# Larger pieces, shared key tiles and late stores in a NaN-ignoring row maximum

## The chip, the cores and the metric

One core of one Trainium2 chip. The metric is the device time of one execution in microseconds (us), the median of the runs given. A difference counts as "faster" or "slower" from 2% on. The span in a profile is about 1.8 us shorter than the device time.

## The reference

```python
# x: 32 x 2048 x 2048 float32, about 10% of it NaN
def reference(x, axis):          # axis = -1
    return np.nanmax(x, axis=axis).astype(np.float32)
```

65,536 rows of 2048 numbers, 8 KB each: 536.87 MB are read, 0.26 MB written. The 128 partitions take 512 rows each.

## The kernel before

A **tile** is 7 rows per partition (7.34 MB) in one of three rotating buffers `xt`. The sync engine (SP) issues its load. Each tile is worked in **pieces** of a few rows: ScalarE (ACT) turns the upper 16 bits of each number into a key in which NaN sorts lowest, into a tile `kt`; GpSimd (POOL), or for a few pieces ACT itself ("back", a minus sign in the list), turns the keys back into numbers in `xt`; VectorE (DVE) takes the maximum of the rows (`reds`). The next load of a buffer waits until DVE has read all of it. The lists in `TILES` give, per tile, the loads, the pieces and the maxima in rows; towards the end they get smaller (the **taper**). A group of tiles shares one result tile and one store.

```python
TILES = (
    [([1], [1], [1])]
    + [([7], [1, 2, 2, -1, 1], [1, 2, 2, 2])] * 59
    # ... 9 tiles of the taper cut
    + [([1, 3, 3], [1, 1, 1, 1, 2, -1], [1, 2, 1, 3])]
    # ... 3 cut
    + [([1, 1, 1, 1, 1, 1, 1], [1, 1, -1, 1, 1, 1, -1], [1, 2, 1, 1, 1, 1])]
)
GROUPS = [TILES[:7]] + [TILES[i : i + 6] for i in range(7, 73, 6)] + [TILES[73:]]
# ... pools: io bufs=3 (xt), mid bufs=4 (kt), res bufs=3 (acc, fin)
        for loads, pieces, reds in g:
            xt = io.tile([P, WIDE * D], i32, tag="xt")
            for c in loads:
                nc.sync.dma_start(out=xt[...], in_=xg[...])
            if len(stores) > 1:
                nc.sync.dma_start(**stores.pop(0))      # a store between two loads
            for c in pieces:
                kt = mid.tile([P, PIECE * D], u16, tag="kt")
                nc.scalar.activation(out=kt, in_=..., func=ACT.Prelu, ...)   # key
                # back on ACT (c < 0) or on POOL
                # ... and every maximum whose rows are complete:
                    nc.vector.tensor_reduce(out=acc[...], in_=xt[...], op=ALU.max)
        # ... end work of the group: none, fin; its store is appended to `stores`
    for st in stores:
        nc.sync.dma_start(**st)
```

Of the kernel before, what the change touches and what calls it, by code (L numbers as in the profile page):

```python
# [1 line left out]

# [4 lines left out]




TILES = (
    [([1], [1], [1])]
    + [([7], [1, 2, 2, -1, 1], [1, 2, 2, 2])] * 59
    + [([7], [2, 2, 1, 2], [4, 1, 2])]
    + [([7], [1, 2, 2, -2], [3, 2, 2])]
    + [([7], [1, 2, 2, 2], [3, 2, 2])]
    + [([7], [2, 2, 2, -1], [2, 2, 2, 1])]
    + [([2, 5], [1, 1, 2, 2, 1], [1, 1, 2, 2, 1])]
    + [([4, 3], [2, -2, 1, 1, 1], [2, 3, 2])]  # L20
    + [([4, 3], [2, 2, 2, -1], [2, 2, 3])] * 3
    + [([1, 3, 3], [1, 1, 1, 1, 2, -1], [1, 2, 1, 3])]
    + [([3, 2, 2], [1, 1, 1, 1, 1, 1, 1], [2, 1, 1, 1, 1, 1])]
    + [([2, 1, 2, 1, 1], [1, 1, -1, 1, 1, 1, 1], [3, 2, 1, 1])]
    + [([1, 1, 1, 1, 1, 1, 1], [1, 1, -1, 1, 1, 1, 1], [3, 1, 1, 1, 1])]
    + [([1, 1, 1, 1, 1, 1, 1], [1, 1, -1, 1, 1, 1, -1], [1, 2, 1, 1, 1, 1])]
)

GROUPS = [TILES[:7]] + [TILES[i : i + 6] for i in range(7, 73, 6)] + [TILES[73:]]
WIDE = 7  # L30
PIECE = 2



TOP = 0x7F7F
NAN = 0x7FC0
LOW = -129

EDGE = TOP + 0.25

NONE = -255.0 * 2.0**120


@with_exitstack
def kernel(
    ctx: ExitStack,
    tc: tile.TileContext,
    x: bass.AP,
    axis: bass.AP,
    out: bass.AP,  # L50
):









    nc = tc.nc
    P = nc.NUM_PARTITIONS
    f32, i32 = mybir.dt.float32, mybir.dt.int32
    i16, u16 = mybir.dt.int16, mybir.dt.uint16
    ALU = mybir.AluOpType
    ACT = mybir.ActivationFunctionType

    nd = len(x.shape)
    assert axis in (-1, nd - 1), axis
    D = x.shape[-1]  # L70

    xr = x.bitcast(i32).flatten_outer_dims()
    R = xr.shape[0]
    of = out.bitcast(i32).flatten_outer_dims().rearrange("r c -> (r c)")
    rows = [sum(sum(loads) for loads, _, _ in g) for g in GROUPS]
    assert R == P * sum(rows)

    io = ctx.enter_context(tc.tile_pool(name="io", bufs=3))
    mid = ctx.enter_context(tc.tile_pool(name="mid", bufs=4))
    res = ctx.enter_context(tc.tile_pool(name="res", bufs=3))  # L80
    sing = ctx.enter_context(tc.tile_pool(name="sing", bufs=1))
    flag = ctx.enter_context(
        tc.tile_pool(name="flag", bufs=2, space=bass.MemoryType.PSUM)
    )
    top = sing.tile([P, 1], f32)
    nc.vector.memset(top, EDGE)  # L86
    warm = sing.tile([P, 1], f32)
    nc.scalar.activation(out=warm, in_=top, func=ACT.Prelu, alpha=0.5)  # L88

    stores = []  # L90
    r0 = 0
    for s, g in zip(rows, GROUPS):
        xg = xr[r0 : r0 + P * s].rearrange("(p s) d -> p (s d)", p=P)
        og = of[r0 : r0 + P * s].rearrange("(p s) -> p s", p=P)
        r0 += P * s
        acc = res.tile([P, s], f32, tag="acc")
        base = 0
        for loads, pieces, reds in g:
            assert sum(loads) == sum(abs(c) for c in pieces) == sum(reds)
            xt = io.tile([P, WIDE * D], i32, tag="xt")  # L100
            at = 0
            for c in loads:
                nc.sync.dma_start(  # L103
                    out=xt[:, at * D : (at + c) * D],
                    in_=xg[:, (base + at) * D : (base + at + c) * D],
                )
                at += c
            if len(stores) > 1:
                nc.sync.dma_start(**stores.pop(0))
            at = done = 0  # L110
            reds = list(reds)
            for c in pieces:
                back, c = c < 0, abs(c)
                xp = xt[:, at * D : (at + c) * D]
                kt = mid.tile([P, PIECE * D], u16, tag="kt")
                nc.scalar.activation(  # L116
                    out=kt[:, : c * D],
                    in_=xp.bitcast(i16)[:, 1::2],
                    func=ACT.Prelu,
                    bias=top,  # L120
                    scale=-1.0,
                    alpha=float(TOP - LOW) / (EDGE - NAN),
                )
                if back:
                    nc.scalar.activation(  # L125
                        out=xp.bitcast(i16)[:, 1::2],
                        in_=kt[:, : c * D],
                        func=ACT.Copy,
                        bias=float(TOP),
                        scale=-1.0,  # L130
                    )
                else:
                    nc.gpsimd.tensor_scalar(  # L133
                        out=xp.bitcast(i16)[:, 1::2],
                        in0=kt[:, : c * D],
                        scalar1=-1.0,
                        scalar2=float(TOP),
                        op0=ALU.mult,
                        op1=ALU.add,
                    )  # L140
                at += c
                while reds and done + reds[0] <= at:
                    n = reds.pop(0)
                    nc.vector.tensor_reduce(  # L144
                        out=acc[:, base + done : base + done + n],
                        in_=xt[:, done * D : (done + n) * D]
                        .bitcast(f32)
                        .rearrange("p (c d) -> p c d", c=n),
                        axis=mybir.AxisListType.X,
                        op=ALU.max,  # L150
                    )
                    done += n
            base += at
        none = flag.tile([P, s], i32, tag="none")
        nc.vector.tensor_scalar(  # L155
            out=none,
            in0=acc,
            scalar1=NONE,
            scalar2=float(0x00C00000),
            op0=ALU.is_equal,  # L160
            op1=ALU.mult,
        )
        fin = res.tile([P, s], i32, tag="fin")
        nc.vector.tensor_tensor(  # L164
            out=fin, in0=acc.bitcast(i32), in1=none, op=ALU.bitwise_or
        )
        stores.append(dict(out=og, in_=fin))
    for st in stores:
        nc.sync.dma_start(**st)


# [1 line left out]
_INS = ['x', 'axis']  # L173
_OUTS = [((32, 2048), 'float32')]

_NUMBERS = {'axis': -1}


# [26 lines left out]
```

## Time and profile before

| | before |
|---|---|
| device time, median of 3 | 1262.26 us (1262.21 to 1262.27) |
| span of the profiled run | 1260.4 us, 1707 instructions |
| DMA engines taken by the main queue | 98.9% of the span |
| busy: DVE, ACT, POOL | 1127.1, 1123.5, 1063.1 us |
| maxima, keys, backs on ACT, backs on POOL | 292, 368, 70, 298 |

The first thing to read is that all three compute engines are 84 to 89% busy and yet none of them is the bound: the DMA row is. A second thing is read from the chain of waits: how long a buffer is **held** after its load has landed (24.1 us), since that decides when its next load can be issued.

### The profile page before, as it was taken

What the parts mean: (1) busy time and instruction counts of PE and PEld (TensorE: products, weight loads), DVE (VectorE), ACT (ScalarE), POOL (GpSimd) and SP (SyncE); (2) the same over time, 40 slices, a digit from 0 to 9 for tenths busy, and PEclk for the clock granted to TensorE, in tenths of its full rate; (3) what the DMA queues carried; (4) which work ended last, traced back from release to release, by engine and by line L of the source; (5) the groups of instructions that cost most, each with busy time, mean ns of one, the idle gap of its engine ahead of it and who ended that gap; (6) DMA issues with size and microseconds to landing.
All of it is one profiled execution on the core that took longest, in us unless ns stands there. A gap on an engine that the chain in (4) does not pass through costs nothing.

```text
span 1260.4 us, 1707 instructions
## 1 busy us (share of the span) xinstructions
DVE 1127.1 (89%) x319; ACT 1123.5 (89%) x440; POOL 1063.1 (84%) x302
## 2 busy tenths in 40 slices
DVE  1899998988989998988999898898989879999999
ACT  4888998888899889889889888998888889899997
POOL 2888888888888888888888888888888888998996
DMA  9999999999999999999999999999999999999995
GB/s 412 437 437 437 435 433 417 434 437 437 436 435 435 427 424 437 436 435 437 435 434 424 426 437 435 437 437 433 435 416 437 437 436 437 417 433 430 425 422 211
DMA packets 16141, 537.25 MB, mean 426 GB/s; under 512 B 3456, under 2 KB 3456, under 8 KB 3456
## 3 DMA queue, kind: packets, MB, share of 16 engines
q1 hardware_dynamic: 16128, 537.14, 98.9%
q14 instruction: 13, 0.11, 0.0%
HBM read 536.87 MB, written 0.26 MB: 426 GB/s over the span
## 4 chain that ended last, share of the span: by engine, by line
DMA 52%; POOL 15%; ACT 13%; DVE 10%; issue 9%; SPq 0%; ACTq 0%; DVEq 0%
DMA xt<-in_x_dram 52%; POOL xt L133 15%; ACT kt L116 12%; DVE acc L144 10%; ACT xt L125 1%; SPq L103 0%; DVE none L155 0%; ACTq L116 0%; DVEq L144 0%; DVE fin L164 0%; ACTq L125 0%
## 5 line engine op out<-in xcount | busy, mean ns | idle before, releaser
L144 DVE TENSOR_REDUCE acc<-xt 128x2 f32<-128x4096 f32 (+2 forms) x292 | 1122.9, 3889 | 129.3 <-POOL xt L133 129.2
L133 POOL TENSOR_SCALAR xt<-kt 128x2048 int16<-128x2048 uint16 (+1 forms) x298 | 1062.9, 3567 | 189.1 <-ACT kt L116 175.7
L116 ACT ACTIVATE kt<-xt,top 128x2048 uint16<-128x2048 int16 (+1 forms) x368 | 951.1, 2657 | 128.4 <-DMA xt<-in_x_dram 128.4
L125 ACT ACTIVATE xt<-kt 128x2048 int16<-128x2048 uint16 x70 | 177.8, 2540 | 0.3
L155 DVE TENSOR_SCALAR none<-acc 128x42 int32<-128x42 f32 (+2 forms) x13 | 2.6, 202 | 0.5
L164 DVE TENSOR_TENSOR fin<-acc,none 128x42 int32<-128x42 int32 (+2 forms) x13 | 2.6, 197 | 0.4
L88 ACT ACT_TABLE_LOAD x1 | 1.3, 1283 | 0.7 <-PEq L186 0.7
L86 DVE MEMSET top<- 128x1 f32 x1 | 0.1, 59 | 0.8 <-PEq L186 0.8
L186 POOL MEMSET const-float32-0.0<- 128x1 f32 x1 | 0.1, 98 | 0.2 <-issue 0.2
L88 ACT ACTIVATE warm<-top 128x1 f32<-128x1 f32 x1 | 0.2, 203 | 0.0
L186 POOL MEMSET const-bfloat16-1.0<- 128x1 bf16 x1 | 0.1, 101 | 0.0
L186 POOL MEMSET const-uint8-127<- 128x1 uint8 x1 | 0.1, 101 | 0.0
L186 POOL MEMSET const-float32-1.0<- 128x1 f32 x1 | 0.1, 98 | 0.0
## 6 DMA issues: line engine op xcount, KB each, us to landing
xt<-in_x_dram SPq DMA_DIRECT2D x63, 7168.0 KB, 26.7
xt<-in_x_dram SPq DMA_DIRECT2D x7, 3072.0 KB, 25.6
xt<-in_x_dram SPq DMA_DIRECT2D x19, 1024.0 KB, 20.8
xt<-in_x_dram SPq DMA_DIRECT2D x4, 4096.0 KB, 19.6
xt<-in_x_dram SPq DMA_DIRECT2D x5, 2048.0 KB, 27.5
xt<-in_x_dram SPq DMA_DIRECT2D x1, 5120.0 KB, 23.2
out_dram<-fin SPq DMA_DIRECT2D x11, 21.0 KB, 26.5
out_dram<-fin SPq DMA_DIRECT2D x1, 21.5 KB, 26.7
```

Source lines behind the costliest of these rows:

```text
L86: nc.vector.memset(top, EDGE)
L88: nc.scalar.activation(out=warm, in_=top, func=ACT.Prelu, alpha=0.5)
L116: nc.scalar.activation(out=kt[:, : c * D], in_=xp.bitcast(i16)[:, 1::2], func=ACT.Prelu, bias=top, scale=-1.0, alpha=float(TOP - LOW) / (E ...
L125: nc.scalar.activation(out=xp.bitcast(i16)[:, 1::2], in_=kt[:, : c * D], func=ACT.Copy, bias=float(TOP), scale=-1.0,)
L133: nc.gpsimd.tensor_scalar(out=xp.bitcast(i16)[:, 1::2], in0=kt[:, : c * D], scalar1=-1.0, scalar2=float(TOP), op0=ALU.mult, op1=ALU.add,)
L144: nc.vector.tensor_reduce(out=acc[:, base + done : base + done + n], in_=xt[:, done * D : (done + n) * D] .bitcast(f32) .rearrange("p (c d ...
L155: nc.vector.tensor_scalar(out=none, in0=acc, scalar1=NONE, scalar2=float(0x00C00000), op0=ALU.is_equal, op1=ALU.mult,)
L164: nc.vector.tensor_tensor(out=fin, in0=acc.bitcast(i32), in1=none, op=ALU.bitwise_or)
L186: nc = _bacc.Bacc("TRN2", target_bir_lowering=False, num_devices=1)
```

## The change

Its intent is to halve the instructions and to take the stores out of the stream of loads. Up to the taper a tile is worked in two pieces of 3 and 4 rows, all turned back by POOL; the key tile holds 4 rows and may be shared by several small pieces, with two buffers instead of four; the 13 groups become 6; all stores are issued behind the last load. Two tiles (the 54th and 55th of seven rows) get lists of their own with a 5-row and a 7-row maximum. Cut to its core:

```diff
-    + [([7], [1, 2, 2, -1, 1], [1, 2, 2, 2])] * 59
+    + [([7], [3, 4], [3, 4])] * 53
+    + [([7], [-1, 3, -1, 2], [5, 2])]
+    + [([7], [4, 2, -1], [7])]
+    + [([7], [3, 4], [3, 4])] * 6
     # ... taper rewritten, same number of tiles
-GROUPS = [TILES[:7]] + [TILES[i : i + 6] for i in range(7, 73, 6)] + [TILES[73:]]
-PIECE = 2
+GROUPS = [TILES[:14]] + [TILES[i : i + 12] for i in range(14, 74, 12)]
+KEYS = 4
 # ...
-            if len(stores) > 1:
-                nc.sync.dma_start(**stores.pop(0))
 # ...
-                kt = mid.tile([P, PIECE * D], u16, tag="kt")
+                if used + c > KEYS:
+                    kt = mid.tile([P, KEYS * D], u16, tag="kt")
+                    used = 0
+                kp = kt[:, used * D : (used + c) * D]
+                used += c
```

(mid goes from 4 to 2 buffers, res from 3 to 1 with a tag per group.)

## The prediction

> **What bounds the kernel now.** I read the page first (the row of bytes moved, the landing times of the transfers), then the groups of instructions by shape, then the waits of the DMA queue, the chain that ended last, and the end of the timeline.
>
> The row of GB/s, of 40 equal slices:
>
> ```profile
> GB/s 412 437 437 437 435 433 417 434 437 437 436 435 435 427 424 437 436 435 437 435 434 424 426 437 435 437 437 433 435 416 437 437 436 437 417 433 430 425 422 211
> ...
> q1 hardware_dynamic: 16128, 537.14, 98.9%
> ...
> xt<-in_x_dram SPq DMA_DIRECT2D x63, 7168.0 KB, 26.7
> ```
>
> The reader is to see a transfer that is never short of work: the 16 DMA engines are taken for 98.9% of the span, and no slice but the first and the last is below 416. 536.87 MB at 437 GB/s are 1228.5 us, of a span of 1260.4. No compute engine can win time in the middle; what is left is the start, a few dips, and the last slice. In the trace's packet records a 7-row load lands every 16.94 us (7.34 MB, 433 GB/s), a store between two loads costs about 0.1 us, and some dips are isolated slow packets (2.1 us in sum). The last load lands near 1244.1.
>
> By shape, the durations that I use:
>
> ```profile
> L144 DVE TENSOR_REDUCE acc<-xt 128x2 f32<-128x4096 f32 x199 | 873.3, 4416 | 95.9 <-POOL xt L133 95.9
> L133 POOL TENSOR_SCALAR xt<-kt 128x4096 int16<-128x4096 uint16 x142 | 676.9, 4767 | 79.5 <-ACT kt L116 73.3
> L116 ACT ACTIVATE kt<-xt,top 128x4096 uint16<-128x4096 int16 x144 | 525.2, 3694 | 8.5 <-DMA xt<-in_x_dram 8.5
> L116 ACT ACTIVATE kt<-xt,top 128x2048 uint16<-128x2048 int16 x224 | 438.2, 1991 | 119.9 <-DMA xt<-in_x_dram 119.9
> L133 POOL TENSOR_SCALAR xt<-kt 128x2048 int16<-128x2048 uint16 x156 | 386.0, 2475 | 109.6 <-ACT kt L116 102.4
> L144 DVE TENSOR_REDUCE acc<-xt 128x1 f32<-128x2048 f32 x83 | 187.9, 2277 | 23.8 <-POOL xt L133 23.8
> L125 ACT ACTIVATE xt<-kt 128x2048 int16<-128x2048 uint16 x68 | 168.3, 2475 | 0.2
> L144 DVE TENSOR_REDUCE acc<-xt 128x3 f32<-128x6144 f32 x9 | 58.9, 6548 | 3.3 <-POOL xt L133 3.2
> ```
>
> Differences of one and two rows give, as an estimate, for n rows: ACT key 0.29 + 1.70n us, POOL way back 0.18 + 2.29n, DVE maximum 0.14 + 2.14n (6.55 at 3 rows, as measured). A piece saved is thus worth only 0.29, 0.18 or 0.14 us.
>
> The chain (start, length) and the queue's own waits:
>
> ```profile
> 80.38 26.64 DMA xt<-in_x_dram
> 107.09 5.61 ACT kt L116 x2
> 131.18 27.00 DMA xt<-in_x_dram
> ...
> SPq L103 <- DVE acc L144: 950.8, 59, 24.1
> SPq L103 <- DVE none L155: 186.6, 11, 21.3
> ```
>
> A load lands at 107.0, and the load that reuses its buffer is issued at 131.2: a tile occupies its buffer for **24.1 us after landing**. With three buffers two other loads, 33.9 us, move meanwhile. From issue to landing are 26.7 us, of which 16.94 are the load's own packets and about 1.3 its start (1.0, below) and its signal (0.3): it queued 8.5 us. That is the margin before the transfer runs dry.
>
> The end:
>
> ```profile
> 1242.32 15.38 DVE L144 TENSOR_REDUCE acc<-xt 128x1 f32<-128x2048 f32 x6
> ...
> 1257.93 0.16 DVE L164 TENSOR_TENSOR fin<-acc,none 128x7 int32<-128x7 int32 x1
> ```
>
> DVE works without a pause to 1257.7, 13.6 us after the last landing: a backlog, not the shortest way of one row, which is 2.0 + 2.5 + 2.3 = 6.8 us. Then 0.36 us of end work and 2.3 us for the last store.
>
> **What the Trainium skill says.** "DMA: Bandwidth & Descriptors", Specifications: 435 GB/s is the fabric's ceiling; the trace agrees (437 in the best slices). The same page, Latency and other measured facts: about 0.6 us to the first byte for a transfer issued by the sync engine; the trace's first load, issued at 0.74, moves its first packet at 1.75, so I use 1.0. "ScalarE: Activation LUTs", What ACT_TABLE_LOAD costs: 280 ns + 0.833 ns per element where the bias is a per-partition operand; the trace agrees (1991 and 3694 ns against 1986 and 3692), so 3 and 4 rows are 5.40 and 7.10. "SBUF — State Buffer", Who interferes with whom: tensor_reduce never contends with GpSimd for the shared port on trn2; the trace agrees, POOL's one-row form takes as long at the end, where DVE never rests, as in the middle. So I leave the durations as they are when both engines are fuller.
>
> **The change, part by part.**
>
> *Fewer pieces.* Counted from the lists: keys 368 to 188, copies back on ACT 70 to 15, POOL 298 to 173, maxima 292 to 166. ACT: 188 x 0.29 + 512 rows x 1.70 + 15 x 2.48 = 963 us (1129 in the groups now). POOL now returns 497 of 512 rows: 173 x 0.18 + 497 x 2.29 = 1170 (1063 now), 93%. DVE: 166 x 0.14 + 512 x 2.14 = 1118 (1123 now). All of it lies beside the transfer: directly 0 us.
>
> *The steady tile* (pieces 3, 4; time from its landing; 0.05 per handover). ACT 3 rows to 5.5, 4 rows to 12.6. POOL 3 rows 5.55 to 12.6, 4 rows 12.65 to 22.0. DVE 3 rows 13.8 (when the tile before is done) to 20.4, 4 rows 22.05 to **30.75**. POOL is busy 16.5 of 16.94 us per tile and frees the second key buffer at 22.0 - 16.94 = 5.06, just before ACT wants it at 5.5. The next load of this buffer moves at 30.75 + 0.05 + 1.0 = 31.8; the DMA is free for it at 33.88 - 0.3 = 33.55. So the margin falls from 8.5 to **1.75 us**, but holds: 0 us.
>
> *Two odd tiles*, the 54th and 55th of seven rows, break it. The order of instructions as built has in the first of them key 1, key 3, back 1, key 1, key 2, back 1 on ACT, ending at 17.95. The 5-row maximum needs that last copy: 18.0 to 28.8, the 2-row one to 33.25. Its buffer's next load moves at 34.3 instead of 33.55: 0.75 lost. In the second, ACT starts 1.0 late, 4 rows to 8.1; POOL 8.15 to 17.5, then 2 rows to 22.3; one 7-row maximum (15.1 us) waits for all: 22.35 to **37.45**. The next load moves at 38.5; the DMA has been free since 33.55 + 0.75 = 34.3: another 4.2 lost. The two tiles after it stay ahead of the late load. Sum: **+5.0 us** of idle DMA, which nothing later can recover, since the transfer has no slack.
>
> *Stores.* Ten that lay between loads go behind the last: 10 x 0.1 = -1.0. Five of the six are ready long before; the last still takes its 2.3. *Loads* of the taper: packet times of 8, 16, 24, 32 KB (0.312, 0.614, 0.915, 1.215 us) with the new counts (12 single rows for 19) give -0.5.
>
> *The end.* I carried the taper tile by tile by the same rules, in the order as built. DVE ends a tile 30.0 us after landing at tile 63 (counted from 0), 29.2 at 64, then about 1.5 less each: 27.6, 26.1, 24.4, 23.0, 21.4, 19.9, 18.5, 17.1 at 72, and **15.5 us** after the last row. (15.2 to 15.9 us of DVE per tile against 16.95 of DMA: the lag shrinks by the difference, and it starts 6.6 higher than now.) As a check: 29.1 (tile 62) + 170.5 of maxima + 3.6 of waits for late copies in tiles 63 and 64 = 203.2, less 187.6 of loads. Now it is 13.6: +1.9. ACT and POOL are done earlier (last copy at 23.1 of a tile whose last landing is 17.4).
>
> Sum: 1262.3 - 1.0 - 0.5 + 5.0 + 1.9 = 1267.7. I say **1266.5**, for the chance that the odd tiles lose less.
>
> **Rivals.**
> 1. *The margin is larger than I think* or the 7-row maximum starts earlier, and the DMA doesn't idle. Then only stores, loads and end count: 1262.7. For it: the loss rests on a start of 1.0 us seen once. Against: 4.2 is far above that uncertainty.
> 2. *POOL becomes the bound.* At 16.5 of 16.94 us, 3% more for its 3- and 4-row forms, which have never been run here, would set the pace: every 0.1 us over 16.94 costs 6 us in 60 tiles, and 0.5 over makes 1292. Against: the line through 1 and 2 rows leaves 0.4, and DVE's 3-row form lies on its line.
> 3. *The buffers run dry at every tile* (30.75 turned into 33 or more). Three tiles then take 33 + 1.35 + 16.94 = 51.3 instead of 50.8, 0.16 per tile: +10, 1277 with the rest.
> 4. *Half the instructions is a gain.* Only if an engine's issue were the bound; ACT waits for the DMA 128 us in all, so no.
>
> **Range and chances.** Rival 1 gives the lower part, isolated slow packets and rival 3 the upper. 1259.5 to 1273 should hold it 8 times in 10. Faster by 2% (under 1237) would need more DMA than its ceiling: 0.01. Slower by 2% (over 1287.5) needs rival 2: 0.04. Within: 0.95.
>
> **What would show it.** Right: loads still every 16.94 us up to the odd tiles; issue to landing about 20 us; one hole of 4 to 5 us in the DMA near 970 us (the load before it lands near 971), one slice there at 370 to 400 GB/s; POOL about 1170 us busy; POOL 3 and 4 rows 7.06 and 9.35; DVE ending 15 to 16 us after the last landing. Wrong: no hole; POOL forms above the line; load pitch above 17.0; DVE's last lag under 10 or over 18.

## The result

| | before | changed |
|---|---|---|
| device time, median of 4 | 1262.26 us | **1296.87 us** (1295.22 to 1297.52) |
| span | 1260.4 us | 1294.7 us |
| instructions | 1707 | 1069 |
| busy: DVE, ACT, POOL | 1127.1, 1123.5, 1063.1 | 1112.7, 954.8, 1169.2 |

Ratio 1.0272, 95% interval 1.0254 to 1.0290: **slower by 2.7%**. (Ratios here are the mean time of one kernel's fast runs over that of the other's of the same rounds, so not quite the ratio of the medians.)

The page of the changed kernel, bytes moved, main queue and time from issue to landing of the 7-row loads:

```profile
GB/s 408 420 445 431 407 432 418 415 423 425 413 411 427 411 434 415 415 438 409 427 422 422 427 402 418 425 420 429 423 407 369 425 422 438 409 427 432 428 424 203
...
q1 hardware_dynamic: 14688, 537.14, 97.8%
...
xt<-in_x_dram SPq DMA_DIRECT2D x63, 7168.0 KB, 21.7
```

Before, most slices stood at 433 to 437; from the fifth on nearly all are now below that. It is not one hole (the one that was predicted is there too, 369) but a loss spread over the whole steady part. And the share of 97.8% says two things: of 1294.7 us the packets took about 1266.2 (before: 98.9% of 1260.4, 1246.5), so they took some 20 us longer for the same bytes, and the engines were idle for some 15 us more. Together that is the 34.3 us by which the span grew.

The engines' work, by shape, is what was predicted (the columns are count, then busy us and mean ns, then idle time before them and what ended it):

```profile
L138 POOL TENSOR_SCALAR xt<-kt 128x8192 int16<-128x8192 uint16 x60 | 559.3, 9321 | 9.2 <-ACT kt L121 4.6
L149 DVE TENSOR_REDUCE acc<-xt 128x4 f32<-128x8192 f32 x60 | 521.1, 8686 | 122.4 <-POOL xt L138 122.4
L138 POOL TENSOR_SCALAR xt<-kt 128x6144 int16<-128x6144 uint16 x63 | 444.7, 7059 | 83.4 <-ACT kt L121 83.2
...
L121 ACT ACTIVATE kt<-xt,top 128x6144 uint16<-128x6144 int16 x63 | 341.0, 5415 | 312.5 <-DMA xt<-in_x_dram 312.5
```

POOL's 3 and 4 rows take 7.06 and 9.32 us, and POOL still sits idle for over 100 us in all. ACT waits for the DMA longer than before, 312.5 us ahead of its 3-row keys alone, where it was 128.4 in all. So no engine became the bound. What became long is the way round, in a piece of the chain of waits (start, length):

```profile
527.88 5.42 ACT kt L121
533.30 0.07 issue
533.38 7.06 POOL xt L138
540.44 0.08 issue
540.52 9.33 POOL xt L138
549.85 0.02 issue
549.87 8.70 DVE acc L149
558.57 0.02 issue
558.59 21.70 DMA xt<-in_x_dram
```

A tile lands at 527.9, its last maximum ends at 558.57 (held 30.7 us, as predicted), its buffer's next load is issued at 558.59 and lands 21.70 us later. The chain closes through the DMA **and** the engines: 30.7 + 21.7 = 52.4 us for three tiles, 17.47 per tile. The mean **pitch** (time from one landing to the next) over loads 3 to 54 is 17.47 (before 17.00). The 21.7 us contain the wait behind the load ahead, so the sum alone proves nothing: before the change it was 24.1 + 26.7 = 50.8, three pitches as well. What has to be found is why the wait no longer absorbs the longer hold. In the timeline of ACT, each start is a landing:

```profile
22.35 12.43 ACT L121 ACTIVATE kt<-xt,top 128x6144 uint16<-128x6144 int16 x2 [14.93 <-DMA xt<-in_x_dram]
39.38 12.43 ACT L121 ACTIVATE kt<-xt,top 128x6144 uint16<-128x6144 int16 x2 [4.61 <-DMA xt<-in_x_dram]
56.30 12.43 ACT L121 ACTIVATE kt<-xt,top 128x6144 uint16<-128x6144 int16 x2 [4.50 <-DMA xt<-in_x_dram]
74.90 12.43 ACT L121 ACTIVATE kt<-xt,top 128x6144 uint16<-128x6144 int16 x2 [6.17 <-DMA xt<-in_x_dram]
```

Two loads follow at 17.0 and 16.9 us (their buffers were free long before), the third, the first that had to wait for a 7-row tile to be given back, at 18.6. The packet records of the trace show what happens to it. (This is a summary of the records, not a view of the profile. The **lead** of a load is the time from its issue to the end of the last packets of the load ahead; it differs among the 16 DMA engines.)

```
load 4, issued 53.02; load 3's last packets end 55.5 to 55.8, so the lead is 2.4 to 2.7 us
   first packet of each of the 16 engines: starts 2.6 to 3.6 us after issue, takes 2.17 to 3.45 us
   second packet:                          takes 2.12 to 2.68 us
   later packets:                          2.12 us
load 5, issued 70.07; load 4's last packets end 73.2 to 74.5, lead 3.1 to 4.4 us
   first packets start 3.1 to 4.4 us after issue and take 2.12 us, like all others
```

The load is in time, in the sense that it has been issued before the one ahead of it ends; but its packets come slowly at first. There is no sharp limit: with the packets of loads 4 to 56 joined end to start into 16 engines (the records do not name the engine), late start and longer packets together cost an engine, as an estimate, 1.4 us per load at leads under 1 us, 0.8 at 1 to 2, 0.4 at 2 to 3, 0.1 at 3 to 3.5 and 0.05 above.

### The profile page after: what moved, and what is told of

Same layout as the page of the kernel before. It is cut to its first block, busy times and chain, and to the rows that moved or that the text cites. A ratio compares the mean times of both kernels' runs of the same rounds, so it can differ in the third digit from the quotient of the medians.

```text
span 1294.7 us, 1069 instructions
## 1 busy us (share of the span) xinstructions
DVE 1112.7 (86%) x179; ACT 954.8 (74%) x205; POOL 1169.2 (90%) x177
## 3 DMA queue, kind: packets, MB, share of 16 engines
q1 hardware_dynamic: 14688, 537.14, 97.8%
## 4 chain that ended last, share of the span: by engine, by line
DMA 40%; POOL 25%; DVE 17%; ACT 13%; issue 5%; ACTq 0%; SPq 0%; DVEq 0%
DMA xt<-in_x_dram 40%; POOL xt L138 25%; DVE acc L149 17%; ACT kt L121 12%; ACT xt L130 1%; ACTq L121 0%; SPq L106 0%; DVE none L160 0%; DVE fin L169 0%; DVEq L149 0%; ACTq L130 0%
## 5 line engine op out<-in xcount | busy, mean ns | idle before, releaser
L138 POOL TENSOR_SCALAR xt<-kt 128x6144 int16<-128x6144 uint16 (+3 forms) x173 | 1169.0, 6757 | 114.4 <-ACT kt L121 106.3
L149 DVE TENSOR_REDUCE acc<-xt 128x3 f32<-128x6144 f32 (+4 forms) x166 | 1110.0, 6728 | 178.3 <-POOL xt L138 169.4
L121 ACT ACTIVATE kt<-xt,top 128x6144 uint16<-128x6144 int16 (+3 forms) x188 | 917.9, 4935 | 330.1 <-DMA xt<-in_x_dram 330.0
L130 ACT ACTIVATE xt<-kt 128x2048 int16<-128x2048 uint16 x15 | 37.2, 2478 | 0.2
## 6 DMA issues: line engine op xcount, KB each, us to landing
xt<-in_x_dram SPq DMA_DIRECT2D x63, 7168.0 KB, 21.7
xt<-in_x_dram SPq DMA_DIRECT2D x7, 3072.0 KB, 22.9
xt<-in_x_dram SPq DMA_DIRECT2D x9, 2048.0 KB, 24.1
```

The lines of the kernel that those rows point to most:

```text
L121: nc.scalar.activation(out=kp, in_=xp.bitcast(i16)[:, 1::2], func=ACT.Prelu, bias=top, scale=-1.0, alpha=float(TOP - LOW) / (EDGE - NAN),)
L130: nc.scalar.activation(out=xp.bitcast(i16)[:, 1::2], in_=kp, func=ACT.Copy, bias=float(TOP), scale=-1.0,)
L138: nc.gpsimd.tensor_scalar(out=xp.bitcast(i16)[:, 1::2], in0=kp, scalar1=-1.0, scalar2=float(TOP), op0=ALU.mult, op1=ALU.add,)
L149: nc.vector.tensor_reduce(out=acc[:, base + done : base + done + n], in_=xt[:, done * D : (done + n) * D] .bitcast(f32) .rearrange("p (c d ...
```

## The experiments

**Theory A**: the time is set by the way round of a buffer: hold plus the time from issue to landing, over three buffers. The hold went from 24.1 to 30.7 us, which leaves a lead of about 2.7 us, and with so short a lead a load starts slowly. **Rivals**: B, POOL's work, 16.5 us per tile, sets the pace; C, the shared key tiles with two buffers, the groups or the stores cost it; D, the two odd tiles are the main cause; E, large pieces are slow in themselves.

### Old lists in the changed code

```diff
 TILES = (
-    # the changed kernel's lists
+    # the lists of the kernel before; KEYS, groups, stores and pools stay changed
```

> The changed kernel with the old lists of pieces and maxima; its six groups, stores behind the last load, shared key tiles and two key buffers are kept. Theory A (a tile keeps its buffer for 30.7 us after landing, so the next load of that buffer is issued too late to start at full speed): the old pieces give 24.1 us back, loads land every 16.94 us, 1261 us. Theory C (the two shared key tiles, the groups or the stores cost the time): about 1297 us.

Measured: 1261.97 us (1261.89 to 1262.21); ratio to before 0.9997 (0.9981 to 1.0014).

```profile
SPq L105 <- DVE acc L148: 1073.8, 66, 24.1
...
xt<-in_x_dram SPq DMA_DIRECT2D x63, 7168.0 KB, 26.7
```

With the old pieces, 26.7 us from issue to landing is back. Rival C falls: shared key tiles, two key buffers, six groups and late stores together cost nothing that this interval (some 2 us to either side) lets one see. The run has the old pieces; that the two key buffers don't hold up the large ones is read from the waits of the changed kernel, where ACT waits for the DMA (330.0 us) and never for a key buffer.

### The 4-row piece cut in two

```diff
-    + [([7], [3, 4], [3, 4])] * 53        # and the * 6
+    + [([7], [3, 2, 2], [3, 2, 2])] * 53
```

> The changed kernel with the 4-row piece and maximum of the steady tile cut into 2 and 2. POOL's work per tile rises from 16.4 to 16.6 us, the hold of a buffer falls from 30.7 to about 28.1 us. Theory A: issue comes over 5 us ahead, loads land every 16.94 us, and 1265 to 1270 us with the hole of the two odd tiles left. Theory B (POOL, 16.5 us per tile, sets the pace): 1300 to 1310 us.

Measured: 1268.07 us (1267.64 to 1268.47), ratio 1.0046. POOL is busy for 1180.4 us, more than in the changed kernel.

```profile
SPq L106 <- DVE acc L149: 1080.0, 66, 27.8
...
xt<-in_x_dram SPq DMA_DIRECT2D x63, 7168.0 KB, 22.9
```

29 us come back with more work on the engine that rival B names: B falls. The longest wait of the DMA queue for a maximum is 27.8 us (30.7 in the changed kernel). The mean pitch of loads 3 to 54 is 16.97 us, and at leads of 3.5 us and more the first packets take 2.12 us. Two pitches, of 18.81 and 20.86 us by the ends of the last packets, are left: 5.8 us over two normal ones, the hole of the odd tiles.

### The pieces in the other order

```diff
-    + [([7], [3, 4], [3, 4])] * 53        # and the * 6
+    + [([7], [4, 3], [4, 3])] * 53
```

> The changed kernel with the steady pieces and maxima in the order 4, 3. Work of every engine is the same; the hold of a buffer rises by about 1.1 us to 31.8. Theory A: three tiles take 1.1 us longer, 20 times: about 1319 us. Theory B (POOL's work sets the pace): unchanged, 1297 us.

Measured: 1315.06 us, one run.

```profile
SPq L106 <- DVE acc L149: 1123.8, 66, 31.7
...
xt<-in_x_dram SPq DMA_DIRECT2D x63, 7168.0 KB, 21.7
```

The same instructions in number and size, 18 us slower. The hold rose by 1.0 to 31.7 us, issue to landing stayed at 21.7: (31.7 + 21.7) / 3 = 17.80, and the mean pitch of loads 3 to 54 is 17.80. This is the strongest support for A: the time from issue to landing did not shrink to absorb the longer hold, as it had from 26.7 to 22.9 in the run with 3, 2, 2, so a microsecond of hold costs a third of a microsecond per tile.

### Two loads per tile

```diff
-    + [([7], [3, 4], [3, 4])] * 53        # and the * 6
+    + [([3, 4], [3, 4], [3, 4])] * 53
```

> The changed kernel with each steady tile loaded by two transfers, 3 rows and 4 rows, into the same buffer. Work of every engine and the count of compute instructions are the same. ACT starts on 3 rows 9.7 us earlier, so the hold after landing falls to about 25.3 us. Theory A: a pitch of 16.95 us per tile, 1262 to 1268 us (the odd tiles still make a hole). Theory B: 1297 us. A theory that larger pieces are slow in themselves: 1297 us.

Measured: 1271.91 us (1271.74 to 1272.43), ratio 1.0077: 25 us back with the same pieces, so large pieces aren't slow in themselves (E falls), but above what I expected. The landings show 7.31 + 9.71 = 17.02 us per tile, 0.08 above one load of 7 rows, which is 5 us over 60 tiles, and two 3-row loads behind the odd tiles that land 8.76 and 11.40 us after the one before in place of 7.31, a hole of 5.5 us. Together that is about the 9.6 us by which the run is slower than before.

### The odd tiles made steady

```diff
-    + [([7], [-1, 3, -1, 2], [5, 2])]
-    + [([7], [4, 2, -1], [7])]
+    + [([7], [3, 4], [3, 4])] * 2
```

> The changed kernel with the two odd tiles (a 5-row and a 7-row maximum) made steady tiles. Theory A: the pitch of the other loads stays at 17.47 us on average and only the extra hole goes, about 4 us by the landings of the changed kernel: 1293 us. If the odd tiles were the main cause: about 1262 us.

Measured: 1293.4 us (1291.15 to 1295.37), ratio 1.0249. About 3.5 us go, as A has it (the runs of each kernel spread over 2 to 4 us, so this is rough), and 31 stay: D is a small part.

### A buffer for each piece

```diff
-    + [([7], [3, 4], [3, 4])] * 53        # and the rest, taper cut alike
+    + [([3], [3], [3]), ([4], [4], [4])] * 53
 # ...
-            xt = io.tile([P, WIDE * D], i32, tag="xt")
+            w = 4 if sum(loads) == 4 else 3
+            xt = io.tile([P, w * D], i32, tag=f"xt{w}")
```

> The changed kernel's steady pieces 3 and 4, but each piece is a tile of its own with its own three buffers and its own load, so that the 3-row buffer is given back when its maximum is done (two odd tiles made steady, taper cut in 3 and 4 rows). Theory A: every load is issued over 10 us ahead, a pitch of 17.02 us for 7 rows (7.31 + 9.71 as two loads take in the run before), and 1262 to 1268 us. Theory B (work of the engines sets the pace) or slow large pieces: 1290 us or more.

Measured: 1265.33 us (1265.15 to 1265.47), ratio 1.0022.

```profile
SPq L102 <- DVE acc L145: 1087.0, 133, 18.7
...
xt<-in_x_dram SPq DMA_DIRECT2D x68, 4096.0 KB, 25.7
xt<-in_x_dram SPq DMA_DIRECT2D x68, 3072.0 KB, 26.5
```

The 3- and 4-row pieces are kept, and the memory too (3 x 3 + 3 x 4 rows); what has changed for A is the moment at which a buffer is given back (loads are also cut in two, the odd tiles made steady and the taper adapted). Loads are now issued some 16 to 19 us ahead, and the loss is gone but for the pitch of two loads (17.05 on average).

### One buffer: the start of a load by itself

```diff
-    io = ctx.enter_context(tc.tile_pool(name="io", bufs=3))
+    io = ctx.enter_context(tc.tile_pool(name="io", bufs=1))
```

> The changed kernel with one buffer in place of three: every load begins with nothing else moving, which measures its start by itself. Prediction's assumption (1.0 us to the first packet, then full speed): 18.3 us from issue to landing of 7 rows. Theory A2 (the first packet of each engine is long as well, 2.7 to 3.3 us for 2.12): 19.5 us. About 3600 us in all either way; the hold after landing stays 30.7 us.

Measured: 3543.93 us, one run, where about 3600 were expected.

```profile
xt<-in_x_dram SPq DMA_DIRECT2D x63, 7168.0 KB, 19.5
```

Into idle DMA engines a 7-row load takes 19.5 us from issue to landing, 1.2 more than the prediction's 18.3. The packet records say where it is: the first packet does start 0.95 us after the issue, but on the last engine 1.3 to 2.2 us after it, and the first packet of each engine takes 2.7 to 3.0 us on average in place of 2.12. This explains only part: 19.5 + 30.7 = 50.2 would still fit in the 50.8 us of three loads. Behind a running load, load 4's first packets started 2.6 to 3.6 us after the issue, later than the 0.95 to 2.2 of idle engines, though its engines were free at 2.4 to 2.7. The packets of two loads are then not merely queued one behind the other; I have no run that shows why.

### Only the stores

```diff
-GROUPS = [TILES[:7]] + [TILES[i : i + 6] for i in range(7, 73, 6)] + [TILES[73:]]
+GROUPS = [TILES[:14]] + [TILES[i : i + 12] for i in range(14, 74, 12)]
-            if len(stores) > 1:
-                nc.sync.dma_start(**stores.pop(0))
```

> The kernel before with only the six groups and all stores behind the last load. Its 10 stores between loads took about 0.1 us each: 1261.3 us, within 0.2% of before by every theory. If stores between loads cost more than that: under 1260 us.

Measured: 1262.04 us (1261.89 to 1262.11), ratio 0.9995 (0.9983 to 1.0008). The gain seen is half a microsecond; the interval holds none, and the predicted 1.0, as well.

### The repaired kernel

```diff
-    + [([7], [3, 4], [3, 4])] * 53
-    + [([7], [-1, 3, -1, 2], [5, 2])]
-    + [([7], [4, 2, -1], [7])]
-    + [([7], [3, 4], [3, 4])] * 6
+    + [([7], [3, 2, 2], [3, 2, 2])] * 61
```

> The changed kernel repaired: steady pieces 3, 2, 2 and the two odd tiles made steady; the rest is the changed kernel's. By theory A both losses are gone: the run with 3, 2, 2 alone gave 1268.1 us, of which 5.8 us are the hole at its tiles 57 and 58 (landings of 18.81 and 20.86 for 33.88): 1262.3 us, equal to before, with 236 instead of 298 POOL and 238 instead of 305 DVE instructions. If the hole has another cause: 1266 to 1268 us.

Measured: 1262.25 us (1262.19 to 1262.35), ratio 1.0000 (0.9986 to 1.0013). Both losses are undone, and the 5.8 us that went with the odd tiles are the size of their hole (the two intervals together leave it uncertain by some 2.5 us). With 1243 instructions for 1707 the time is the same: fewer instructions gain nothing here.

### Another taper

```diff
     + [([7], [1, 2, 2, -1, 1], [1, 2, 2, 2])] * 59
-    # the old taper
+    + [([7], [1, 1, 1, 2, 2], [1, 1, 3, 2])]
+    # ... 12 tiles with smaller loads, cut
+    + [([1, 1, 1, 1, 1, 1, 1], [1, 1, -1, 1, 1, 1, -1], [2, 2, 1, 2])]
```

> The kernel before with all stores behind the last load and another taper (smaller loads and pieces from 10 tiles before the end, other copies back). The only part of the time that no run has shown to be the DMA's is DVE's backlog of 13.6 us behind the last landing, for 6.8 us that one row needs. The taper is to bring the backlog to about 10 or 11 us: 1259 to 1260 us. If the end isn't set by this backlog: 1262 us.

Measured: 1262.83 us (1262.78 to 1263.07), ratio 1.0005: a miss. The premise was misread. The last load of the kernel before lands at 1248.2, not near 1244.1: between 1244 and 1248 the 16 DMA engines are busy for only 0.20 of the time, but the last packets end at 1247.75, and ACT gets the signal for its last key at 1248.2. The backlog was thus 9.5 us, of which one row needs 6.8. In DVE's timeline, the new taper has these two as its longest waits:

```profile
1039.38 15.41 DVE L144 TENSOR_REDUCE acc<-xt 128x3 f32<-128x6144 f32 x3 [3.04 <-POOL xt L133]
...
1075.91 24.31 DVE L144 TENSOR_REDUCE acc<-xt 128x2 f32<-128x4096 f32 x9 [2.26 <-POOL xt L133]
```

The kernel before had these:

```profile
1038.51 15.21 DVE L144 TENSOR_REDUCE acc<-xt 128x4 f32<-128x8192 f32 x3 [6.28 <-POOL xt L133]
...
1211.27 30.66 DVE L144 TENSOR_REDUCE acc<-xt 128x3 f32<-128x6144 f32 x9 [2.12 <-POOL xt L133]
```

All waits of DVE from 1030 on come to 10.9 us with the new taper and 10.8 before: they were moved, not removed. The maxima end at 1257.9, 10.1 us after the last landing at 1247.9, so the backlog wasn't brought down. No version here beats the kernel before by more than its noise.

## Why the prediction was wrong, point by point

- **The bound and the hold were right.** The hold was predicted as 30.75 us and measured as 30.7. POOL's 3 and 4 rows: 7.06 and 9.35 predicted, 7.06 and 9.32 measured; POOL 1170 and 1169.2 busy. DVE's 5 and 7 rows: 10.8 and 15.1 both. Half the instructions gained nothing.
- **The step that failed** is "The next load of this buffer moves at 30.75 + 0.05 + 1.0 = 31.8; the DMA is free for it at 33.88 - 0.3 = 33.55. So the margin falls from 8.5 to 1.75 us, but holds: 0 us." Its mechanism was the right one, and so was the lead that it implies: 33.55 - 30.80 = 2.75 us, measured 2.4 to 2.7 at load 4. The term "1.0" for the start of a load, which that lead had to cover, was mis-sized. I took it from the first load of the trace, of one row, up to its first packet. Into idle engines a 7-row load takes 19.5 us from issue to landing, where 0.05 + 1.0 + 16.94 + 0.3 = 18.3 were assumed. Behind a running load, **a lead of 2.4 to 2.7 us was too short**: load 4 lost 1.8 us. Loads 5 and 6, with leads of 3.1 us and more, lost nothing. Over the steady part, hold and issue to landing come to 30.7 + 21.7 = 52.4 us, against 50.8 us of DMA for three tiles: no margin of 1.75, but a lack of 1.6 us every third tile. Loads 4 to 63 are twenty such rounds, 32 us; the run without the odd tiles, 31 us slower than before, shows this part by itself. Why a load with a short lead starts so slowly stays open.
- **Rival 3** ("30.75 turned into 33 or more") had the right formula and the wrong start: it put 1.35 us on the start and signal, and so a loss of 10 us. It also looked for the excess in the hold, where there was none. The case "slower by over 2%" was tied to rival 2, POOL as the bound; the runs with 3, 2, 2 and with 4, 3 refute that.
- **The odd tiles**: 5.0 us predicted. Removing them gave 5.8 us where the rest of the kernel left the DMA a lead (1268.07 - 1262.25), 3.5 us in the changed kernel. Right in size and place (the slice of 369 GB/s).
- **The stores**: -1.0 predicted; about half of it seen, within the noise.
- **The end**: DVE was to end 15.5 us after the last row, +1.9 against a backlog of 13.6. The 13.6 rests on the misread landing (1248.2 in place of 1244.1, see the last run): it was 1257.7 - 1248.2 = 9.5 us. In the changed kernel the last load lands at 1280.0, and the maxima end at 1291.6:

```profile
1278.44 13.18 DVE L149 TENSOR_REDUCE acc<-xt 128x1 f32<-128x2048 f32 x5
...
1291.93 0.24 DVE L169 TENSOR_TENSOR fin<-acc,none 128x84 int32<-128x84 int32 x1
```

That is 11.7 us, +2.2 against before. The difference came out about right; the level of 15 to 16 us, given as a sign, did not.

## What to carry to other kernels

In a kernel bound by transfers, compute engines with time to spare can still set the time through the buffers. Subtract the hold from the time in which the loads of the other buffers move: what is left is the lead of the next load. Ask whether it covers the start of a load behind a running one, and take that start from such a load, not from the first load of the trace. Don't judge by hold plus issue-to-landing in a running kernel: the second contains the wait in the queue, so with three buffers the sum is three pitches whatever the margin. Larger pieces lengthened the hold here (24.1 us with the old pieces, 27.8 with 3, 2, 2, 30.7 with 3, 4), since the last piece passes the engines one after the other; keep the last piece small, or give each part its own buffer. Leave several microseconds of lead: here 2.4 to 2.7 us was too short, and 3.5 us and more cost next to nothing.

## What the Trainium skill lacked or had wrong

- "DMA: Bandwidth & Descriptors", Latency and other measured facts: about 0.6 us to the first byte. Here the first packet starts 0.95 us after the start of the issuing instruction; that instruction takes 0.33 us, so counted from its end the figure agrees (0.62), but the page does not say from where it counts. And it isn't the whole start: the last engine's first packet starts 1.3 to 2.2 us after the issue, and first packets of 57,344 B take 2.7 to 3.0 us on average in place of 2.12. A 7-row load takes 19.5 us from issue to landing for 16.94 us of moving.
- No page that I read says how far ahead of the end of a running load the next one must be issued to follow at full speed. Here a lead of 2.4 to 2.7 us lost 1.8 us (load 4: a pitch of 18.7 for 16.9, by the ends of the last packets), 3.1 us and more lost nothing at loads 5 and 6, and 3.5 us and more next to nothing in all loads.
- No page that I read says that a load issued shortly before another ends can start later than one into idle engines: 2.6 to 3.6 us after the issue at load 4, whose engines were free at 2.4 to 2.7, against 0.95 to 2.2 us into idle engines. The cause is open.
- "SBUF — State Buffer", Summary: rules for kernel authors, says to estimate HBM to SBUF at about 358 GB/s. This core, alone, moved 437 GB/s in its best slices and 426 over the span, near the 435 that the DMA page gives as the fabric's ceiling. Another page of the skill says that a core alone exceeds its share; this rule does not.
